# The end of a transformer block's kernel: sums put into PSUM one step sooner, a shorter inverse root, centring read from PSUM

## The chip, the cores and the metric

The kernel runs on one core of one Trainium2 chip. The metric is the device time of one execution in microseconds (us). The kernel before was timed three times: 1820.85 us in the median, 1820.63 us at the lowest and 1821.01 us at the highest. One more execution was taken with the hardware profiler; all rows shown here come from it.

## The reference

256 tokens of width 1024, all in float32, go through two blocks one after the other. The first is a mixer of three attentions and a gated feed-forward layer; the second has two layers: a gated recurrence with a dense feed-forward layer, then differential attention with a mixture of experts. Only the end of the second layer of the second block bears on the change:

```python
y = moe_swiglu(h, w_router, w_gate, w_up, w_down)   # 8 experts, 2 of them for each token
h = layer_norm(DEEPNORM_ALPHA * h + y, ln_g[layer, 1], ln_b[layer, 1])

def layer_norm(x, g, b):
    mu = jnp.mean(x, axis=-1, keepdims=True)
    xc = x - mu
    var = jnp.mean(xc * xc, axis=-1, keepdims=True)
    return xc * lax.rsqrt(var + 1e-5) * g + b
```

An expert computes `(silu(x @ w_gate) * (x @ w_up)) @ w_down` for its tokens, with 3584 hidden features.

## The kernel before, in words

All weights come from HBM as one stream of 1 MB tiles (`wr`, 128 x 2048), in the order in which they are used; SyncE issues the loads (line 266) into slots that the users of earlier tiles set free. The last tile of the stream comes as four loads of 256 KB.

The experts are the last part of the program. Four of them ("heavies", `expert`) have room for 128 tokens, the four others ("lights", `expert_few`, lines 1586 to 1663) for 64. Both kinds run beside each other in a fixed order of turns; what runs last is the last light expert, alone. In the stretch of the experts and the final norm the order of the instructions of TensorE (PE), VectorE (DVE), ScalarE (ACT) and SyncE (SP) is the order in which the code issues them (`manual_schedule(engines=ALL)`), and each engine runs its list in that order.

A light expert goes through seven chunks of 512 hidden features, c = 0 to 6, and one closing round, c = 7:

- gate and up products of chunk c, PSUM bank `gu` (line 1620, 64 matmul records on PE for one chunk), then `hidden` (lines 1414 to 1419): Silu on ACT and a product on DVE, tile `sg`;
- `features` of the chunk before (line 1606): `sg` is turned by PE into PSUM (`uT`), and ACT copies it to `uf` (line 1608). In rounds 1 to 6 this is issued after the first quarter of the gate and up products, in round 7 at the round's start;
- the down product of the chunk before (line 1644, 16 matmul records), added up in bank `dn`.

So round 6 holds the gate and up products of chunk 6 and the down product of chunk 5, and round 7 the down product of chunk 6.

`macc` (128 x 2 x 1024, in SBUF) holds ALPHA times the layer's input plus what all experts gave so far. In the last light expert the sum is closed in PSUM: four matmuls with the identity put the four blocks of 128 x 512 of `macc` into four banks `sum` (lines 1634 to 1639, in round 7 between `features` and the down product). After the down product ACT scales `dn` to `ye` (line 1649), and four matmuls (line 1654, 8 records) add the expert's part into the same banks, each token to its row. DVE takes statistics of each bank (line 1657, `fst`), and ACT copies each bank back to `macc` (line 1658).

`normed` (lines 1710 to 1726) is the final layer norm: `mv` is mean and variance for both token tiles. `inv_sqrt` (lines 440 to 456) computes 1/sqrt(variance + eps) on DVE alone for 128 x 2 values: a first guess by integer operations (lines 446, 447) and three Newton steps of three small instructions each (lines 453 to 455). Between them stand the four centring instructions (line 1717), (macc - mean) * gain, into `done` (a free weight slot, hence `wr` in the trace). Then four instructions multiply by the root and add the bias (line 1724), each followed by a store of 128 x 512 to HBM (line 1726). Gain and bias come by two loads (line 398) into another free weight slot.

If an expert has more tokens than room, a second pass (`again`) runs at the end, and `normed` once more from `macc`. None of its instructions shows in the trace.

Of the kernel before, what the change touches and what calls it, by code (L numbers as in the profile page):

```python
# [10 lines left out]
F32 = mybir.dt.float32  # L11
# [339 lines left out]
def tile_kernel(ctx: ExitStack, tc: tile.TileContext, cst, par, wst, x, mem, g_mix, g_mem, g_ffn, w_forget,  # L351
# [87 lines left out]

    def inv_sqrt(m, eps, between):  # L440


        v, r, w = (mo.tile([128, 2], F32, name=n) for n in ("iv", "ir", "iw"))
        i = mo.tile([128, 2], I32, name="ii")
        V.tensor_scalar(out=v, in0=m, scalar1=eps, scalar2=None, op0=ALU.add)
        V.tensor_scalar(out=i, in0=v.bitcast(I32), scalar1=1, scalar2=None, op0=ALU.logical_shift_right)
        V.tensor_scalar(out=i, in0=i, scalar1=-1.0, scalar2=float(0x5f3759df), op0=ALU.mult, op1=ALU.add)
        r0 = i.bitcast(F32)
        for step in range(4):
            between[step]()  # L450
            if step == 3:
                return r
            V.tensor_tensor(w, r0, r0, op=ALU.mult)
            V.scalar_tensor_tensor(out=w, in0=w, scalar=-0.5, in1=v, op0=ALU.mult, op1=ALU.mult)
            V.scalar_tensor_tensor(out=r, in0=w, scalar=1.5, in1=r0, op0=ALU.add, op1=ALU.mult)
            r0 = r
# [957 lines left out]
    def hidden(pg, pu):  # L1414

        sg = sm.tile([128, 512], F32, name="sg", tag="sq", bufs=2)[:, 0:pg.shape[-1]]
        A.activation(out=sg, in_=pg, func=AF.Silu)
        V.tensor_tensor(sg, sg, pu, op=ALU.mult)
        return sg
# [175 lines left out]
    def expert_few(s, late, last=False):  # L1595
# [15 lines left out]
        for c in range(8):  # L1611
            end = c == 7
            if not end:
# [12 lines left out]
                turn = hidden(ps[:, 0], ps[:, 1])  # L1626
# [6 lines left out]
            if end and last:  # L1633

                for t in range(2):
                    for n in range(2):
                        summed.append(pa("sum"))
                        T.matmul(summed[-1], ident, macc[:, t, n * 512:n * 512 + 512], start=True, stop=False)
# [12 lines left out]
        def scatter(t):  # L1651
            pss = summed[2 * t:2 * t + 2] or [pb("sp") for _ in range(2)]
            for n, h in enumerate(halves):
                T.matmul(pss[n], PT[h, t], y[h], start=not last, stop=True)
            for n in range(2):
                if last:
                    V.bn_stats(out=fst[:, t, n], in_=pss[n])
                    A.activation(out=macc[:, t, n * 512:n * 512 + 512], in_=pss[n], func=AF.Copy)
                else:
                    added(t, n, pss[n], False)  # L1660
# [3 lines left out]
    left = {}  # L1664
# [45 lines left out]
    def normed():  # L1710
# [3 lines left out]

        def centred(t, c):
            cc = slice(c * 512, c * 512 + 512)
            return lambda: V.scalar_tensor_tensor(out=done[:, t, cc], in0=macc[:, t, cc], scalar=mv[:, t, 0:1],
                                                  in1=gbf[:, cc], op0=ALU.subtract, op1=ALU.mult)

        r = inv_sqrt(mv[:, :, 1], 1e-5, [centred(t, c) for t in range(2) for c in range(2)])  # L1720
        for t in range(2):
            for c in range(2):
                cc = slice(c * 512, c * 512 + 512)
                V.scalar_tensor_tensor(out=done[:, t, cc], in0=done[:, t, cc], scalar=r[:, t:t + 1], in1=bbf[:, cc],
                                       op0=ALU.mult, op1=ALU.add)
                nc.sync.dma_start(out=out[t * 128:t * 128 + 128, cc], in_=done[:, t, cc])
# [28 lines left out]
    with tc.manual_schedule(engines=ALL):  # L1755
# [3 lines left out]
        normed()  # L1759

    most = nc.values_load(cint[0:1, 0:1], min_val=0, max_val=S)
    with tc.If(most > 0):
        again()
        with tc.manual_schedule(engines=MS):
            normed()
# [33 lines left out]
```

## Time and profile before

| | |
|---|---|
| median of three runs | 1820.85 us |
| the profiled execution | 1820.72 us |
| its span, first to last instruction or transfer in the trace | 1818.6 us |
| PE busy | 1777.8 us, 98% of the span |
| DVE busy | 1103.4 us, 61% |
| ACT busy | 867.8 us, 48% |
| weights and other data by DMA | 512.70 MB |
| the last instruction on PE ends | about 1803.4 us |
| the last instruction on DVE ends | 1813.05 us |

The profiled execution's own time is 2.12 us more than its span, and 0.13 us under the median of the runs. Engines other than PE are busy for half of the time, so for nearly the whole program they run beside PE. A 128 x 512 product of float32 data shows as two records of PE. "Idle before" in a row is the time in which the engine stood before the instruction, and the name behind the arrow is what ended it.

### The profile page before, as it was taken

The page shows a single profiled execution, that of the slowest core. Times are in us where ns is not written, and L with a number is a line of the kernel's source. Part 1 is how long each engine was busy: PE and PEld are TensorE (multiplying, and loading weights), DVE is VectorE, ACT ScalarE, POOL GpSimd, SP SyncE. Part 2 cuts the span into 40 slices and gives each one's busy share as a digit, 9 for nine tenths or more (in the row PEclk, how much of TensorE's full clock was granted, in tenths as well). Part 3 has the DMA queues.
Part 4 walks back from the last instruction along what each step waited for, and adds up shares of the span by engine and source line. Part 5 has one row for each costly group of instructions (what it writes and reads, how often), then busy time and mean ns, then how long its engine had stood idle before and what let it go on. Part 6 is the DMA issues. An engine that isn't in the chain of part 4 may idle for free.

```text
span 1818.6 us, 27621 instructions
## 1 busy us (share of the span) xinstructions
PE 1777.8 (98%) x11150; PEld 1427.3 (78%) x11150; DVE 1103.4 (61%) x1609; ACT 867.8 (48%) x1222; POOL 0.2 (0%) x4
## 2 busy tenths in 40 slices
PE   8999999999999999999999999999999999999996
PEld 6898998999899899987787767776777677766662
DVE  7856756555676955569789464746464645664622
ACT  6675655444433454436547344545453534553521
POOL 0000000000000000000000000000000000000000
PEclk9999999999999999999999999999999999999998
DMA  7533455555433465534647699999999999999995
GB/s 266 184 140 139 146 193 196 199 206 186 169 137 131 172 235 197 194 140 181 229 173 292 255 420 420 419 420 419 419 419 420 419 419 419 419 419 418 409 419 220
DMA packets 73287, 512.70 MB, mean 282 GB/s; under 512 B 8512, under 2 KB 9152, under 8 KB 12096
## 3 DMA queue, kind: packets, MB, share of 16 engines
q1 hardware_dynamic: 73152, 510.86, 71.2%
q8 instruction: 89, 1.46, 0.3%
q14 instruction: 46, 0.38, 0.1%
HBM read 509.78 MB, written 1.05 MB: 281 GB/s over the span
## 4 chain that ended last, share of the span: by engine, by line
PE 79%; DMA 11%; DVE 7%; ACT 2%; issue 1%; SPq 0%; DVEq 0%; ACTq 0%
DMA wr<-in_wst_dram 10%; PE gu L1620 8%; PE fm L482 7%; PE fm L493 7%; PE fm L486 7%; PE gu L482 5%; PE gu L484 5%; PE gu L491 5%; PE dn L1644 4%; PE acc L484 3%; PE acc L482 3%; PE acc L491 3%; DVE wl L309 3%; PE tk L484 3%; PE tk L482 3%; PE tk L491 3%
## 5 line engine op out<-in xcount | busy, mean ns | idle before, releaser
L309 DVE TENSOR_TENSOR wl<-wr,wh 128x1024 fp32r<-128x1024 f32 x620 | 729.7, 1220 | 366.1 <-ACT wh L307 352.9
L307 ACT ACTIVATE wh<-wr 128x1024 fp32r<-128x1024 f32 x620 | 617.4, 1051 | 315.7 <-PE fm L486 91.3
L482 PE MATMUL fm<-xh,wh 128*128 128x256 f32 x1056 | 251.5, 280 | 0.0
L486 PE MATMUL fm<-xl,wh 128*128 128x256 f32 x1056 | 249.6, 278 | 0.0
L1620 PE MATMUL gu<-wr,xfew 128*64 128x256 f32 x1792 | 208.2, 385 | 0.0
L482 PEld LDWEIGHTS fm<-xh,wh 128*128 128x128 f32 x1056 | 198.8, 188 | 1.1 <-issue 0.2
L486 PEld LDWEIGHTS fm<-xl,wh 128*128 128x128 f32 x1056 | 198.7, 188 | 0.9
L1620 PEld LDWEIGHTS gu<-wr,xfew 128*64 128x64 f32 x1792 | 124.9, 138 | 77.5 <-issue 21.9
L482 PE MATMUL gu<-wh,xe 128*128 128x512 f32 (+1 forms) x448 | 178.3, 399 | 0.0
L484 PE MATMUL gu<-wh,xe 128*128 128x512 f32 (+1 forms) x448 | 173.7, 389 | 0.0
L493 PE MATMUL fm<-xh,wl 128*128 128x256 f32 x1056 | 145.4, 278 | 0.0
L493 PEld LDWEIGHTS fm<-xh,wl 128*128 128x128 f32 x1056 | 131.6, 188 | 0.0
L491 PE MATMUL gu<-wl,xe 128*128 128x512 f32 (+1 forms) x448 | 120.0, 390 | 0.4 <-DVE wl L309 0.4
L482 PE MATMUL tk<-wh,xh 128*128 128x512 f32 x288 | 115.7, 402 | 1.7 <-ACT wh L307 1.5
L484 PE MATMUL tk<-wh,xl 128*128 128x512 f32 x288 | 113.5, 394 | 0.5 <-DVE xl L464 0.5
L482 PEld LDWEIGHTS gu<-wh,xe 128*128 128x128 f32 x448 | 84.5, 189 | 31.7 <-ACT wh L307 11.7
L1608 ACT ACTIVATE uf<-uT 128x256 f32<-128x256 f32 x28 | 10.7, 384 | 203.9 <-PE uT L1606 203.9
L1644 PE MATMUL dn<-wr,uf 128*64 128x512 f32 x448 | 103.0, 594 | 1.9 <-ACT uf L1608 1.4
L491 PEld LDWEIGHTS gu<-wl,xe 128*128 128x128 f32 x448 | 83.6, 189 | 19.2 <-DVE wl L309 1.1
L484 PEld LDWEIGHTS gu<-wh,xe 128*128 128x128 f32 x448 | 84.5, 189 | 16.6 <-DVE xe L464 0.3
L482 PE MATMUL dn<-wh,uh 128*128 128x512 f32 x224 | 89.2, 398 | 0.0
L484 PE MATMUL dn<-wh,ul 128*128 128x512 f32 x224 | 88.0, 393 | 0.0
(347 smaller groups left out, 2214.7 us busy)
## 6 DMA issues: line engine op xcount, KB each, us to landing
wr<-in_wst_dram SPq DMA_DIRECT2D x477, 1024.0 KB, 12.1
gb<-in_ln_g_dram SPq DMA_DIRECT2D x3, 512.0 KB, 5.7
gb<-in_ln_b_dram SPq DMA_DIRECT2D x3, 512.0 KB, 6.5
memt<-in_mem_dram SPq DMA_DIRECT2D x2, 512.0 KB, 7.3
res<-in_x_dram SPq DMA_DIRECT2D x2, 512.0 KB, 12.9
wr<-in_wst_dram SPq DMA_DIRECT2D x4, 256.0 KB, 15.5
out_dram<-wr SPq DMA_DIRECT2D x4, 256.0 KB, 3.0
gb<-in_g_mem_dram SPq DMA_DIRECT2D x1, 512.0 KB, 5.1
```

The lines of the kernel that those rows point to most:

```text
L307: self.nc.scalar.activation(out=h[:, c], in_=t[:, c], func=AF.Copy)
L309: return [lambda c=c: self.nc.vector.tensor_tensor(l[:, c], t[:, c], h[:, c].bitcast(F32), op=ALU.subtract) for c in cols]
L482: T.matmul(ps, ah, bh, start=first and i == 0, stop=False)
L484: T.matmul(ps, al, bh, start=False, stop=False)
L486: T.matmul(ps, ah, bl, start=False, stop=False)
L491: T.matmul(ps, ah, bl, start=False, stop=last and i == n - 1)
L493: T.matmul(ps, al, bh, start=False, stop=last and i == n - 1)
L1608: A.activation(out=U, in_=pT, func=AF.Copy)
L1620: T.matmul(ps[h, g], xfew[:, u + k, i * FEW:i * FEW + FEW], w[:, k, 256 * b:256 * b + 256], start=u + k == 0, stop=u + k == KD - 1)
L1644: T.matmul(acc[h], U[:, j, b * FEW:b * FEW + FEW], wd[n][:, k], start=c == 1 and k == 0, stop=end and k == 3)
```

## The change

Four edits, all at the end of the program.

1. In the last light expert the four identity matmuls that put `macc` into the banks `sum` are issued in round 6, between the gate and up products of chunk 6 and the down product of chunk 5, and no longer in round 7. The first of the four banks comes from the other pool of PSUM (`pb` in place of `pa`), since chunk 6 still holds a bank of `pa`.
2. `hidden` of chunk 6 is followed on ACT by the load of the function table that holds Ln and Exp (`LOGEXP`).
3. The inverse root is exp(-0.5 * ln(v)) by two instructions on ACT, and one Newton step on DVE. The integer guess and two Newton steps go.
4. The four centring instructions read the banks `sum` in place of `macc`, and stand in a row before the Newton step. ACT's four copies of the banks to `macc` come after `normed`.

```diff
--- before.py
+++ after.py
@@ -437,24 +437,6 @@
         V.tensor_tensor(w, w, r, op=ALU.mult)
         return w
 
-    def inv_sqrt(m, eps, between):
-
-
-        v, r, w = (mo.tile([128, 2], F32, name=n) for n in ("iv", "ir", "iw"))
-        i = mo.tile([128, 2], I32, name="ii")
-        V.tensor_scalar(out=v, in0=m, scalar1=eps, scalar2=None, op0=ALU.add)
-        V.tensor_scalar(out=i, in0=v.bitcast(I32), scalar1=1, scalar2=None, op0=ALU.logical_shift_right)
-        V.tensor_scalar(out=i, in0=i, scalar1=-1.0, scalar2=float(0x5f3759df), op0=ALU.mult, op1=ALU.add)
-        r0 = i.bitcast(F32)
-        for step in range(4):
-            between[step]()
-            if step == 3:
-                return r
-            V.tensor_tensor(w, r0, r0, op=ALU.mult)
-            V.scalar_tensor_tensor(out=w, in0=w, scalar=-0.5, in1=v, op0=ALU.mult, op1=ALU.mult)
-            V.scalar_tensor_tensor(out=r, in0=w, scalar=1.5, in1=r0, op0=ALU.add, op1=ALU.mult)
-            r0 = r
-
     def urgent():
 
         return tc.high_priority(offset=PRIO)
@@ -1411,10 +1393,12 @@
         mm3(ps, [((X5[0][:, k, tk], X5[1][:, k, tk]), (w[0][:, k], w[1][:, k])) for k in range(KD)])
         return ps
 
-    def hidden(pg, pu):
+    def hidden(pg, pu, final=False):
 
         sg = sm.tile([128, 512], F32, name="sg", tag="sq", bufs=2)[:, 0:pg.shape[-1]]
         A.activation(out=sg, in_=pg, func=AF.Silu)
+        if final:
+            A.preload_act_table_set(LOGEXP)
         V.tensor_tensor(sg, sg, pu, op=ALU.mult)
         return sg
 
@@ -1623,18 +1607,18 @@
                             U = features(turn)
                         if late and c == 0:
                             late.pop(0)()
-                turn = hidden(ps[:, 0], ps[:, 1])
+                turn = hidden(ps[:, 0], ps[:, 1], last and c == 6)
             else:
                 U = features(turn)
             if c == 0:
                 acc = pb("dn")
             if c == 3:
                 PT, gs = back([[few[:, t, i]] * 2 for t in range(2)], s, F32, "PU")
-            if end and last:
+            if c == 6 and last:
 
                 for t in range(2):
                     for n in range(2):
-                        summed.append(pa("sum"))
+                        summed.append((pb if t + n == 0 else pa)("sum"))
                         T.matmul(summed[-1], ident, macc[:, t, n * 512:n * 512 + 512], start=True, stop=False)
             if c:
                 wd = [W.get_whole(), W.get_whole()]
@@ -1655,13 +1639,13 @@
             for n in range(2):
                 if last:
                     V.bn_stats(out=fst[:, t, n], in_=pss[n])
-                    A.activation(out=macc[:, t, n * 512:n * 512 + 512], in_=pss[n], func=AF.Copy)
+                    sums.append(pss[n])
                 else:
                     added(t, n, pss[n], False)
 
         return [lambda: scatter(0), lambda: scatter(1)]
 
-    left = {}
+    left, sums = {}, []
 
     def heavies(Pm, begun):
         late = []
@@ -1707,23 +1691,25 @@
 
     mv = mo.tile([128, 2, 2], F32, name="mv")
 
-    def normed():
+    def normed(part):
 
         for t in range(2):
             V.bn_aggr(out=mv[:, t], in_=fst[:, t])
-
-        def centred(t, c):
-            cc = slice(c * 512, c * 512 + 512)
-            return lambda: V.scalar_tensor_tensor(out=done[:, t, cc], in0=macc[:, t, cc], scalar=mv[:, t, 0:1],
-                                                  in1=gbf[:, cc], op0=ALU.subtract, op1=ALU.mult)
-
-        r = inv_sqrt(mv[:, :, 1], 1e-5, [centred(t, c) for t in range(2) for c in range(2)])
-        for t in range(2):
-            for c in range(2):
-                cc = slice(c * 512, c * 512 + 512)
-                V.scalar_tensor_tensor(out=done[:, t, cc], in0=done[:, t, cc], scalar=r[:, t:t + 1], in1=bbf[:, cc],
-                                       op0=ALU.mult, op1=ALU.add)
-                nc.sync.dma_start(out=out[t * 128:t * 128 + 128, cc], in_=done[:, t, cc])
+        v, r, w = (mo.tile([128, 2], F32, name=n, tag=n) for n in ("iv", "ir", "iw"))
+        V.tensor_scalar(out=v, in0=mv[:, :, 1], scalar1=1e-5, scalar2=None, op0=ALU.add)
+        A.activation(out=r, in_=v, func=AF.Ln)
+        A.activation(out=r, in_=r, func=AF.Exp, scale=-0.5)
+        cols = [(t, slice(n * 512, n * 512 + 512), part(t, n)) for t in range(2) for n in range(2)]
+        for t, cc, ps in cols:
+            V.scalar_tensor_tensor(out=done[:, t, cc], in0=ps, scalar=mv[:, t, 0:1], in1=gbf[:, cc], op0=ALU.subtract,
+                                   op1=ALU.mult)
+        V.tensor_tensor(w, r, r, op=ALU.mult)
+        V.scalar_tensor_tensor(out=w, in0=w, scalar=-0.5, in1=v, op0=ALU.mult, op1=ALU.mult)
+        V.scalar_tensor_tensor(out=r, in0=w, scalar=1.5, in1=r, op0=ALU.add, op1=ALU.mult)
+        for t, cc, ps in cols:
+            V.scalar_tensor_tensor(out=done[:, t, cc], in0=done[:, t, cc], scalar=r[:, t:t + 1], in1=bbf[:, cc],
+                                   op0=ALU.mult, op1=ALU.add)
+            nc.sync.dma_start(out=out[t * 128:t * 128 + 128, cc], in_=done[:, t, cc])
 
     with tc.manual_schedule(engines=MS):
         tail(0)
@@ -1756,13 +1742,15 @@
         experts(Pm, [s0, s1])
         gbf, bbf = bcast2(W.spare(), 1, 1)
         done = W.spare().rearrange("p (t c) -> p t c", t=2)
-        normed()
+        normed(lambda t, n: sums[2 * t + n])
+        for i, ps in enumerate(sums):
+            A.activation(out=macc[:, i // 2, i % 2 * 512:i % 2 * 512 + 512], in_=ps, func=AF.Copy)
 
     most = nc.values_load(cint[0:1, 0:1], min_val=0, max_val=S)
     with tc.If(most > 0):
         again()
         with tc.manual_schedule(engines=MS):
-            normed()
+            normed(lambda t, n: macc[:, t, n * 512:n * 512 + 512])
 
 
 def arrange(inputs):
```

The list of PE around the end of the last light expert, before (`gu` gate and up products, `uT` the turning of a chunk's features, `dn` the down product, `sum<-macc` the identity matmuls, `sum<-ye` the adding of the expert's part):

```order
L1606 MATMUL uT<-cs,sg 128x128 x2
L1620 MATMUL gu<-wr,xfew 64x256 x24
L1644 MATMUL dn<-wr,uf 64x512 x8
L1606 MATMUL uT<-cs,sg 128x128 x2
L1638 MATMUL sum<-macc,cs 128x512 x4
L1644 MATMUL dn<-wr,uf 64x512 x8
L1654 MATMUL sum<-ye,PU 128x512 x4
```

The same place of PE's list in the changed kernel, where line numbers are 16 lower:

```order
L1590 MATMUL uT<-cs,sg 128x128 x2
L1604 MATMUL gu<-wr,xfew 64x256 x24
L1622 MATMUL sum<-macc,cs 128x512 x4
L1628 MATMUL dn<-wr,uf 64x512 x8
L1590 MATMUL uT<-cs,sg 128x128 x2
L1628 MATMUL dn<-wr,uf 64x512 x8
L1638 MATMUL sum<-ye,PU 128x512 x4
```

The four identity matmuls moved ahead of the first down product shown, past it and past the turning `uT`; nothing else on PE moved, and all that stands earlier in the program is as before.

The end of ACT's list in the changed kernel, from the Silu of chunk 6 on (`ir<-iv` is Ln, `ir<-ir` is Exp):

```order
L1399 ACTIVATE sg<-gu 128x256
L1401 ACT_TABLE_LOAD
L1592 ACTIVATE uf<-uT 128x256
L1633 ACTIVATE ye<-dn,gs 128x512
L1700 ACTIVATE ir<-iv 128x2
L1701 ACTIVATE ir<-ir 128x2
L1747 ACTIVATE macc<-sum 128x512 x4
```

Before, the table load and the two small instructions were not there, and the four copies followed `ye` directly.

## Rows read from the trace of the kernel before

**Rows 1.** The page: span, and busy time of PE with its share and count.

```profile
span 1818.6 us, 27621 instructions
...
PE 1777.8 (98%) x11150; PEld 1427.3 (78%) x11150; DVE 1103.4 (61%) x1609; ACT 867.8 (48%) x1222; POOL 0.2 (0%) x4
```

**Rows 2.** Chain of work that ended last, from 1785 us: start, length, what.

```profile
1772.64 16.88 DMA wr<-in_wst_dram
...
1797.02 3.63 PE dn L1644 x16
```

**Rows 3.** Timeline of the last light expert: start, length, engine, what, count, idle before.

```profile
1775.89 3.60 PE L1644 MATMUL dn<-wr,uf 128*64 128x512 f32 x16
...
1779.42 0.50 PE L1521 MATMUL sp<-yy,PT 128*128 128x512 f32 x1
...
1788.02 1.02 PE L1644 MATMUL dn<-wr,uf 128*64 128x512 f32 x2
1788.65 0.42 DVE L1418 TENSOR_TENSOR sg<-sg,gu 128x256 f32<-128x256 f32 x1 [7.18 <-ACT sg L1417]
1789.56 0.20 PEld L1644 LDWEIGHTS dn<-wr,uf 128*64 128x64 f32 x4 [1.41 <-DMA wr<-in_wst_dram]
...
1793.14 0.44 PE L1606 MATMUL uT<-cs,sg 128*128 128x128 f32 x2
...
1793.42 3.60 PE L1638 MATMUL sum<-macc,cs 128*128 128x512 f32 x8
1793.68 0.38 ACT L1608 ACTIVATE uf<-uT 128x256 f32<-128x256 f32 x1 [5.06 <-PE uT L1606]
...
1796.95 3.65 PE L1644 MATMUL dn<-wr,uf 128*64 128x512 f32 x16
...
1800.68 0.69 ACT L1649 ACTIVATE ye<-dn,gs 128x512 f32<-128x512 f32 x1 [6.61 <-PE dn L1644]
...
1801.41 1.99 PE L1654 MATMUL sum<-ye,PU 64*128 64x512 f32 x8 [0.81 <-ACT ye L1649]
```

**Rows 4.** DMA issue at 1781.96 us: last weights, KB, us to landing.

```profile
wr<-in_wst_dram SPq DMA_DIRECT2D x1, 256.0 KB, 12.7
```

**Rows 5.** Stretches: us, busy time by engine, PE clock granted, DMA share, GB/s.

```profile
1788.00:1793.00 5.00, 4.48 (x18) 1.18 (x15) 0.42 (x1) 0.38 (x1) 0.00 (x0) 1.00 1.02 397
...
1801.00:1804.00 3.00, 1.99 (x8) 0.69 (x8) 1.43 (x3) 1.05 (x3) 0.00 (x0) 1.00 0.02 5
```

**Rows 6.** Timeline of the final norm.

```profile
1802.58 2.49 DVE L1657 BATCH_NORM_STATS2 fst<-sum 128x6 f32<-128x512 f32 x4 [13.50 <-PE sum L1654]
1803.31 2.39 ACT L1658 ACTIVATE macc<-sum 128x512 f32<-128x512 f32 x4 [1.95 <-DVE fst L1657]
...
1805.35 0.17 DVE L445 TENSOR_SCALAR iv<-mv 128x2 f32<-128x2 f32 x1
...
1805.75 0.17 DVE L447 TENSOR_SCALAR ii<-ii 128x2 int32<-128x2 int32 x1
1806.28 0.75 DVE L1717 SCALAR_TENSOR_TENSOR wr<-macc,mv,wr 128x512 f32<-128x512 f32 x1 [0.36 <-issue]
1806.95 0.15 DVE L453 TENSOR_TENSOR iw<-ii 128x2 f32<-128x2 f32 x1
...
1807.33 0.16 DVE L455 SCALAR_TENSOR_TENSOR ir<-iw,ii 128x2 f32<-128x2 f32 x1
1807.41 0.75 DVE L1717 SCALAR_TENSOR_TENSOR wr<-macc,mv,wr 128x512 f32<-128x512 f32 x1
...
1810.32 2.73 DVE L1724 SCALAR_TENSOR_TENSOR wr<-wr,ir 128x512 f32<-128x512 f32 x4
```

**Rows 7.** DVE group by shape: busy us, mean ns, idle before, releaser.

```profile
L1514 DVE SCALAR_TENSOR_TENSOR yy<-dn,gs,yy 128x512 fp32r<-128x512 f32 x8 | 6.0, 751 | 19.0 <-ACT yy L1513 19.0
```

**Rows 8.** Groups of ACT by shape: small functions and table loads.

```profile
L1417 ACT ACT_TABLE_LOAD x2 | 2.6, 1283 | 0.0
...
L428 ACT ACTIVATE nr<-nv 128x1 f32<-128x1 f32 x12 | 2.4, 201 | 26.3 <-DVE nv L427 26.3
```

## The prediction, made before the changed kernel had run

> **What bounds the kernel now.** I read the page first, then the chain of waits at the end, then the timeline of the last 45 us, because the change touches nothing earlier. PE is busy for 98% of the span of 1818.6 us [rows 1]. So the program is bound by PE's list while that list runs, and what comes behind it, on other engines, lies bare on the end. The chain of waits shows both: until 1789.5 us the chain is a weight load, then PE to the end of the last down product (3.63 us from 1797.02 us on) [rows 2], and from there a relay of ACT, PE and DVE with one engine at work at a time. The reader should see in the timeline that the end has three parts: PE's list to about 1800.6 us, the relay over `ye` and the last matmuls to the statistics at 1802.58 us, and DVE alone from there to 1813.05 us [rows 3, 6]. After that come the last store and the closing, 1818.6 - 1813.05 = 5.55 us of the span, which I leave as they are.
>
> **The sums one step sooner (PE).** In round 6 the gate and up products end and the first down matmul starts at 1788.02 us. It stops after one of its eight matmuls, because the second weight tile is not there: PE's weight loading waits for a DMA and goes on at 1789.56 us [rows 3]. The whole down product of round 6 takes 1793.14 - 1788.02 = 5.12 us from its start to the start of what follows, where the same block one round earlier takes 1779.42 - 1775.89 = 3.53 us [rows 3]. So the wait costs 1.59 us. The identity matmuls take 1796.95 - 1793.42 = 3.53 us from start to start [rows 3]. Put at 1788.02 us they run until 1791.55 us, two microseconds beyond the landing of that tile, and the whole wait is covered.
>
> What is lost is the cover that they gave in round 7. There the chunk's turning starts at 1793.14 us, the identity matmuls 0.28 us later, and ACT's copy `uf` (start 0.54 us after the turning's start, 0.38 us long) is done long before the down product needs it at 1796.95 us [rows 3]. In the changed list the down product follows the turning directly and must wait for that copy. The hop from ACT's end to PE's start I take from `ye`: it ends at 1801.37 us and the next matmul starts at 1801.41 us [rows 3], 0.04 us. So turning to down product: 0.54 + 0.38 + 0.04 = 0.96 us, where 0.28 us is all that the turning took before; 0.68 us are added.
>
> New times: sums 1788.02 to 1791.55, down product 1791.55 to 1795.08, turning at 1795.08, last down product at 1796.04 us. Before it started at 1796.95 us, so **0.91 us** are gained (1.59 - 0.68). The last weights are in place: their last load is issued at about 1782 us and lands 12.7 us later, at 1794.7 us [rows 4], 1.3 us ahead of the new start. Bounds of this term: nothing, if the sums cannot start where they now stand (a rival below), and 1.59 us, if the new hop cost nothing.
>
> The table load takes 1.28 us [rows 8]. It stands on ACT between the Silu of chunk 6, whose product DVE starts at 1788.65 us [rows 3], and `uf`, which is not due before 1795.6 us in the new order, so the 7 us of idle ACT hide it. Without that cover it would delay `uf` and so the down product by 1.28 us.
>
> **The root and the centring (DVE).** From `iv` (the variance plus eps) at 1805.35 us to the end of the last instruction at 1810.32 + 2.73 = 1813.05 us DVE needs 7.70 us now [rows 6]. By parts:
> - The two integer instructions: from `iv` to the second of them 1805.75 - 1805.35 = 0.40 us [rows 6]. They go.
> - In front of the first centring DVE stands 0.36 us for nothing that the trace shows [rows 6]. In the list this instruction waits for gain, bias and slot by three DMA signals and for ACT's copy; in the new kernel the three DMA signals remain. I keep the 0.36 us. Bounds: it goes altogether, or stays.
> - Each centring takes 0.67 us until the next instruction starts (1806.28 to 1806.95), each Newton step 0.46 us more (1806.95 to 1807.41) [rows 6]. Four centrings stay. Two Newton steps go, 2 x 0.46 = 0.92 us.
> - The remaining step's third instruction was followed at once by a centring that does not use it, 0.08 us after its start (1807.33 to 1807.41). Now the next instruction uses its result, which costs a whole pitch of small instructions, about 0.19 us (the two between 1806.95 and 1807.33) [rows 6]. Added: 0.11 us.
>
> Sum 0.40 + 0.92 - 0.11 = **1.21 us**.
>
> Ln and Exp lie beside the centrings. `iv` ends at 1805.52 us on the old clock; a small function on ACT takes 0.20 us [rows 8], so with hops of some 0.04 us the root is there about 0.5 us after `iv`. DVE wants it only after four centrings, 0.36 + 4 x 0.67 = 3.0 us after `iv`. There are 2.5 us of slack, more than even a second table load of 1.28 us.
>
> The centrings now read PSUM. The nearest row is the same form of instruction, 128 x 512 with its first input in PSUM: 751 ns [rows 7], against 0.75 us for the centring from SBUF [rows 6]. I take no difference. [...]
>
> ACT's copies to `macc` were waited for by the centrings and now wait for them: that ACT waits for DVE bank by bank shows already before (1.95 us behind the statistics [rows 6]). The last copy starts when the fourth centring ends, some 3.3 us after `iv`, and takes 0.6 us (2.39 us for four [rows 6]); DVE ends 6.5 us after `iv`. So nothing waits for them, unless the output pass became 2.5 us shorter.
>
> **Sum.** 0.91 + 1.21 = 2.12 us less than the profiled execution's 1820.72 us: 1818.6 us. That execution lies 0.13 us under the median of the runs, so I forecast **1818.7 us**, a gain of 0.12%. About 0.2%, 3.6 us, is what a measurement of this kernel can tell from no change, so the forecast lies within it.
>
> **Rivals.**
> - The sums start late. If the first bank `sum` were one that chunk 6 still holds, its first matmul would wait for that chunk's product on DVE, 1788.65 + 0.42 = 1789.07 us [rows 3], that is 1.05 us after its place; the gain of 0.91 us is gone and only the norm gains: 1820.85 - 1.21 + 0.14 = 1819.8 us. Against it: the first bank comes from the other pool, and the other three from banks of earlier chunks. In the same way the gain on PE goes if the last weights land 2 us later than now. Chance 0.08.
> - Only PE gains, the norm does not: if the wait for Ln and Exp outlasted the centrings by 1.2 us, that is, if ACT took 4.2 us for what I put at 0.5. 1820.85 - 0.91 = 1819.9 us. Chance 0.04.
> - More than forecast: the 0.36 us in front of the centring go too, and the hop to the last down product overlaps the turning. 1818.7 - 0.36 - 0.5 = 1817.8 us. To reach 0.2% another 0.6 us would be needed, for which I see no row. Chance 0.12 for clearly more gain, of which a third beyond 0.2%.
> - Slower: PE's clock falls in the new hop. PE now has a gap of some 0.5 us between the turning and the last down product. [...] Against it: through the DMA wait of round 6, which is longer, and through the 0.81 us before the last matmuls the granted clock stays at 1.00 [rows 3, 5]. [...] Chance 0.02.
>
> **How the numbers follow.** The forecast has 0.74: both gains as worked out, within half a microsecond (1818.2 to 1819.3). The range should hold 8 of 10: with the page's price for PSUM, the loss of the DVE gap of 0.36 us, either gain alone (1819.8, 1819.9) and the stronger case (1817.8), it goes from 1817.8 to 1819.9 us. Faster by over 0.2% (below 1817.2 us): 0.05. Slower by over 0.2% (above 1824.5 us) would need the clock rival in full and something besides: 0.01. Within 0.2%: 0.94.
>
> **What would show it.** In the profile after: the DMA wait before the weight loading of round 6 is gone from PE and eight records of identity matmuls stand in its place; the last down product starts about 0.9 us sooner, with a wait for ACT's `uf` of about half a microsecond before it; the table load lies between Silu and `uf`, with ACT idle behind it; Ln and Exp lie under the first centring; DVE goes from `iv` to its end in about 6.5 us with no wait for ACT's root; the four centrings take about 0.75 us each. I am wrong if the sums wait for a bank, if the centrings from PSUM take visibly longer than 0.75 us, or if a wait for ACT appears in front of the Newton step.

## The result: 11 us slower, and none of it where the change is

The changed kernel takes 1832.09 us (median of 5 runs, 1829.50 to 1832.68); the kernel before took 1820.85 us (1820.09 to 1821.08) beside it. The ratio is 1.0059, interval [1.0045, 1.0073]. The forecast was 1818.7 us, so the sign is wrong.

First the page of the kernel after: span, and busy time of PE.

```profile
span 1830.3 us, 27616 instructions
...
PE 1797.8 (98%) x11150; PEld 1438.9 (79%) x11150; DVE 1102.8 (60%) x1601; ACT 866.8 (47%) x1225; POOL 0.2 (0%) x4
```

Beside [rows 1]: PE has the same 11150 matmuls, but they are busy for 1797.8 us instead of 1777.8, 20.0 us more. PE's idle time fell from 1818.6 - 1777.8 = 40.8 us to 1830.3 - 1797.8 = 32.5 us, 8.3 us less. 20.0 - 8.3 = 11.7 us is the whole difference of the spans. The change neither adds nor enlarges a matmul; something made the old ones slower.

**The end, where the change is.** The timeline of the last light expert and of the norm, after (start, length, engine, line, what, count, idle before):

```profile
1802.22 3.70 PE L1622 MATMUL sum<-macc,cs 128*128 128x512 f32 x8
...
1802.74 1.28 ACT L1401 ACT_TABLE_LOAD   x1
...
1805.85 3.65 PE L1628 MATMUL dn<-wr,uf 128*64 128x512 f32 x16
...
1809.44 0.44 PE L1590 MATMUL uT<-cs,sg 128*128 128x128 f32 x2
...
1810.41 3.65 PE L1628 MATMUL dn<-wr,uf 128*64 128x512 f32 x16 [0.53 <-ACT uf L1592]
...
1818.81 0.17 DVE L1699 TENSOR_SCALAR iv<-mv 128x2 f32<-128x2 f32 x1
1818.91 2.73 DVE L1704 SCALAR_TENSOR_TENSOR wr<-sum,mv,wr 128x512 f32<-128x512 f32 x4
1819.01 0.20 ACT L1700 ACTIVATE ir<-iv 128x2 f32<-128x2 f32 x1 [4.18 <-DVE iv L1699]
...
1819.70 2.57 ACT L1747 ACTIVATE macc<-sum 128x512 f32<-128x512 f32 x4 [0.25 <-DVE wr L1704]
...
1821.56 0.15 DVE L1706 TENSOR_TENSOR iw<-ir 128x2 f32<-128x2 f32 x1
...
1822.13 2.74 DVE L1710 SCALAR_TENSOR_TENSOR wr<-wr,ir 128x512 f32<-128x512 f32 x4
```

The reader is to see that the end looks as predicted: the sums run at once, the table load lies under them, Ln stands under the first centring, no wait for ACT stands before the Newton step. From the place where the lists part (down product before, sums after) to DVE's end it was 1813.05 - 1788.02 = 25.03 us [rows 3, 6] and is 1824.87 - 1802.22 = 22.65 us: **2.38 us less**, 2.12 were forecast. But that place is reached 1802.22 - 1788.02 = **14.2 us later**. With 0.1 us less for the closing, 14.2 - 2.4 - 0.1 = 11.7 us.

**Upstream, where it came from.** The loads of ACT's tables mark the same points of the program in both traces. Before, in the timeline of ACT:

```profile
295.43 1.28 ACT L631 ACT_TABLE_LOAD   x1
...
793.94 1.28 ACT L422 ACT_TABLE_LOAD   x1
...
964.56 1.28 ACT L1417 ACT_TABLE_LOAD   x1
```

After:

```profile
298.06 1.28 ACT L613 ACT_TABLE_LOAD   x1
...
807.27 1.28 ACT L422 ACT_TABLE_LOAD   x1
...
978.94 1.28 ACT L1399 ACT_TABLE_LOAD   x1
```

The delay is 2.6 us, then 13.3, then 14.4. It grows with the work of PE, not at one wait. The groups by shape name the work; before (busy us, mean ns of one, idle before):

```profile
L482 PE MATMUL fm<-xh,wh 128*128 128x256 f32 x1056 | 251.5, 280 | 0.0
L486 PE MATMUL fm<-xl,wh 128*128 128x256 f32 x1056 | 249.6, 278 | 0.0
...
L493 PE MATMUL fm<-xh,wl 128*128 128x256 f32 x1056 | 145.4, 278 | 0.0
```

After:

```profile
L464 PE MATMUL fm<-xh,wh 128*128 128x256 f32 x1056 | 257.6, 282 | 0.0
L468 PE MATMUL fm<-xl,wh 128*128 128x256 f32 x1056 | 255.8, 281 | 0.0
...
L475 PE MATMUL fm<-xh,wl 128*128 128x256 f32 x1056 | 149.0, 281 | 0.0
```

These are the gate and up products of the two feed-forward layers, and the same form of product in projections beside them (split inputs `xh`, `xl`, streamed through PE, against weights `wh`, `wl`, loaded into it): 15.9 of the 20.0 us. A block of eight of them in the timeline of PE, before:

```profile
370.99 1.07 PE L493 MATMUL fm<-xh,wl 128*128 128x256 f32 x8
```

and after:

```profile
370.32 1.10 PE L475 MATMUL fm<-xh,wl 128*128 128x256 f32 x8
```

The last record of a block lasts 0.28 us, so seven pitches (a pitch is the time from one product's start to the next) are 0.79 us before (113 ns each) and 0.82 us after (117 ns). From the starts of single records in the feed-forward layers I read 113.3 ns before and 117.3 ns after, in all three groups and with no idle time between. The simplest view of it is how many matmuls fit into a stretch in which PE does the feed-forward's products without a pause. 300 to 460 us, PE's busy time and count in the second and third place, granted clock near the end; before:

```profile
300.00:460.00 160.00, 160.00 (x1175) 150.31 (x1175) 85.17 (x83) 73.81 (x84) 0.00 (x0) 1.00 0.56 202
```

After:

```profile
300.00:460.00 160.00, 160.00 (x1151) 150.19 (x1150) 81.88 (x82) 70.75 (x82) 0.00 (x0) 1.00 0.57 202
```

PE is busy for all 160 us in both, the granted clock is 1.00 in both, DMA moves the same 202 GB/s: 24 matmuls fewer, 2%. This count serves as the mark below.

Of the 8.3 us of PE's idle time that went, 2.4 went ahead of the last of these table loads (13.7 us of idle time before, 11.3 after), 4.2 between it and the place where the lists part (10.6 and 6.4), and 1.8 in the end itself. The largest single piece lies among the experts, between 1640 and 1680 us. That stretch, and PE's timeline at one place in it, before:

```profile
1640.00:1680.00 40.00, 37.38 (x180) 24.18 (x179) 17.99 (x19) 14.34 (x17) 0.00 (x0) 0.91 1.01 419
...
1655.72 2.67 PE L1654 MATMUL sp<-ye,PU 64*128 64x512 f32 x4 [2.15 <-DVE macc L1483]
1658.32 6.05 PE L1620 MATMUL gu<-wr,xfew 128*64 128x256 f32 x32
```

After:

```profile
1640.00:1680.00 40.00, 39.44 (x212) 25.25 (x209) 24.80 (x26) 19.79 (x25) 0.00 (x0) 1.00 1.01 418
...
1673.35 3.67 PE L1604 MATMUL gu<-wr,xfew 128*64 128x256 f32 x32
```

DMA is full at 419 and 418 GB/s (share 1.01 in both); before, PE stood 2.6 us here, after, 0.6. Of the 2.6, 2.15 us are a wait for DVE; before it DVE had stood 13.2 us for ACT, and ACT 1.9 us for a weight load. From 1600 to 1700 us ACT's waits for weight loads add up to 8.7 us before and 2.2 after. So here the later PE waited less for what comes by DMA.

The two stretches differ in one thing more: the mean granted clock is 0.91 before and 1.00 after, and the 32 products behind that wait take 6.05 us before and 3.67 after (granted clock 0.50 from 1658 to 1661 us before, 1.00 from 1673 to 1678 us after). So of the time that the changed kernel makes up here, 2.4 us go with the lower granted clock. The lower clock does not go with the change: the group of these products, `gu<-wr,xfew`, takes 384 or 385 ns a record in the traces of the kernel before and of experiments 5, 8 and 12 below, and 382 ns in those of the changed kernel and of experiments 1, 2, 3, 4, 6, 7 and 10.

**What differs there.** The instructions are the same; their addresses are not. The traces hold no addresses; the compiled programs do. The old root needs an integer tile `ii` (128 x 2, in the pool of the router and the norm, where it takes 32 bytes of each partition). The new root has none, so all that is placed behind this pool lies 32 bytes lower: `xh` at byte 118,464 instead of 118,496, and with it `xl` and what shares their places. The weights `wh`, `wl` stay (`wh` at 43,040). The distance from stationary weights to streamed inputs falls from 75,456 to 75,424 bytes, that is from 192 to 160 modulo 256. The other buffers of `xh`, `xl`, `wh` and `wl` lie multiples of 256 bytes from these.

### The profile page after: what moved, and what is told of

Read it like the earlier page. It is cut to its first block, busy times and chain, and to the rows that moved or that the text cites. A ratio compares the mean times of both kernels' runs of the same rounds, so it can differ in the third digit from the quotient of the medians.

```text
span 1830.3 us, 27616 instructions
## 1 busy us (share of the span) xinstructions
PE 1797.8 (98%) x11150; PEld 1438.9 (79%) x11150; DVE 1102.8 (60%) x1601; ACT 866.8 (47%) x1225; POOL 0.2 (0%) x4
## 4 chain that ended last, share of the span: by engine, by line
PE 92%; DVE 5%; ACT 1%; issue 1%; DMA 0%; SPq 0%; DVEq 0%; ACTq 0%
PE gu L1604 10%; PE fm L464 7%; PE fm L475 7%; PE fm L468 7%; PE gu L464 6%; PE gu L466 6%; PE gu L473 6%; PE dn L1628 5%; PE acc L466 3%; PE acc L464 3%; PE acc L473 3%; PE tk L466 3%; PE tk L473 3%; PE tk L464 3%; PE dn L464 3%; PE dn L473 3%
## 5 line engine op out<-in xcount | busy, mean ns | idle before, releaser
L464 PE MATMUL fm<-xh,wh 128*128 128x256 f32 x1056 | 257.6, 282 | 0.0
L468 PE MATMUL fm<-xl,wh 128*128 128x256 f32 x1056 | 255.8, 281 | 0.0
L473 PEld LDWEIGHTS gu<-wl,xe 128*128 128x128 f32 x448 | 83.6, 189 | 20.8 <-DVE wl L309 0.8
## 6 DMA issues: line engine op xcount, KB each, us to landing
res<-in_x_dram SPq DMA_DIRECT2D x2, 512.0 KB, 12.9
```

What stands on the lines that cost most here:

```text
L464: T.matmul(ps, ah, bh, start=first and i == 0, stop=False)
L468: T.matmul(ps, ah, bl, start=False, stop=False)
L473: T.matmul(ps, ah, bl, start=False, stop=last and i == n - 1)
```

## The experiments

**Theory:** the distance in SBUF between the streamed and the stationary operand sets PE's pitch in these products. **Rivals:** the code itself (other instructions at the end, or where the instructions lie); the absolute address of the inputs; the weights or another tile that moved along. Ratios are against the kernel before, run on the same chip.

**1. The changed kernel with 32 bytes put back.**

```diff
     mv = mo.tile([128, 2, 2], F32, name="mv")
+    mo.tile([128, 8], F32, name="pad")
```

> The changed kernel with 32 unused bytes per partition in the place where the integer tile `ii` of the old root lay, so that every operand of PE lies in SBUF where it lay before; no instruction differs from the changed kernel. Theory A (the loss is a matter of where tiles lie in SBUF: without `ii` all tiles behind it lie 32 bytes lower, and PE's products run slower from there): the slow products are gone, the fm products are back at 113 to 114 ns, and only the gain of the end is left, 25.03 - 22.65 = 2.4 us between the start of the stretch behind the last gate and up products and the end of DVE, so 1820.85 - 2.4 = 1818.4 us (1817.8 to 1819.2). Theory B (the loss comes from the changed instructions or the changed program as such, wherever tiles lie): about 1832 us, as the changed kernel.

Measured: 1818.57 us, ratio 0.9983 [0.9974, 0.9992]; the pitch is 113.3 ns. The stretch of the feed-forward:

```profile
300.00:460.00 160.00, 160.00 (x1183) 150.62 (x1181) 84.35 (x83) 74.31 (x86) 0.00 (x0) 1.00 0.57 206
```

The unused tile takes 13.5 us off the changed kernel, and what is left is the gain at the end. (1183 in place of the 1175 of the kernel before, at the same pitch: the count also goes by which products fall into the stretch.) No instruction differs from the changed kernel's.

**2. The kernel before without its integer tile** (the bits of the root go to an old 8-column tile that is free by then).

```diff
-        i = mo.tile([128, 2], I32, name="ii")
+        i = i8[:, 0, 0:2].bitcast(I32)
```

> The kernel before with nothing changed but that the integer guess of the root is kept in a tile that the routing no longer needs, so that `ii` is not allocated and all tiles behind it lie 32 bytes lower, as in the changed kernel. Theory A (place in SBUF): about 1832.1 + 2.4 = 1834.5 us (1831 to 1836), fm products at 115 to 120 ns. Theory B (the changed instructions): 1820.85 us, within 0.5 us.

Measured: 1834.07 us, ratio 1.0078 [1.0064, 1.0091]; pitch 117.25 ns.

```profile
300.00:460.00 160.00, 160.00 (x1151) 150.19 (x1150) 81.83 (x82) 70.82 (x82) 0.00 (x0) 1.00 0.56 202
```

The same 1151 matmuls as in the changed kernel, with the old end. So no edit at the end is needed for the loss, and the code rival falls.

**3 and 4. Distance or address.** A tile of 32 bytes ahead of all, in the pool of constants, moves weights and inputs alike. In the changed kernel it puts the inputs back to their old addresses and the weights 32 bytes above theirs (the new distance stays); in the kernel before it moves both up (the old distance stays).

```diff
     causb = const.tile([128, 128], BF16, name="causb")
+    const.tile([128, 8], F32, name="pad")
```

Changed kernel:

> The changed kernel with 32 unused bytes per partition ahead of the weight tiles, so that the whole layout behind the constants moves up: the inputs of the products (xh, xl) lie where they lay before, the weight halves (wh, wl) 32 bytes higher than before; the distance between them is that of the changed kernel. Theory A1 (what counts is where the streamed inputs themselves start): 1818.4 us, fm products at 113 to 114 ns. Theory A2 (what counts is the distance between the streamed input and the stationary weights): about 1832 us, fm products at 115 to 120 ns.

Measured: 1831.28 us, ratio 1.0055 [1.0039, 1.0070], 1150 matmuls in the stretch.

Kernel before:

> The kernel before with 32 unused bytes per partition ahead of the weight tiles: inputs and weights of the products all 32 bytes higher, the distance between them as before. Theory A1 (the start of the streamed inputs counts; here it lies 64 bytes above that of the changed kernel): slow, about 1834 us. Theory A2 (the distance counts): 1820.85 us, within 0.7 us. If the step of 32 bytes matters in neither way, also 1820.85 us, and the experiment with the inputs back in place tells the two apart.

Measured: 1820.16 us, ratio 0.9995 [0.9986, 1.0004], 1175 matmuls. Inputs at their old address are slow when the weights have moved, and both moved alike are as fast as ever. The absolute address falls, the distance stands.

**5 and 6. The two halves of the change, each at the old distance.** The sums alone, in the kernel before:

```diff
-            if end and last:
+            if c == 6 and last:
 ...
-                        summed.append(pa("sum"))
+                        summed.append((pb if t + n == 0 else pa)("sum"))
```

> The kernel before with the first edit alone (the identity matmuls in round 6, the first bank from the other pool); the root and the norm as before, and all tiles where they were. By the step of the prediction: the wait of 1.59 us for a weight tile is covered and a hop of 0.68 us is added, so 0.9 us less: 1820.85 - 0.9 = 1820.0 us against 1820.85 us on the same chip, and in the profile the last down product starts 4.6 us after the turning of round 6's end less the sums, that is 8.0 us after the gate and up products end (before: 8.9 us). The rival that the sums start late: no gain, and a gap in front of the first identity matmul.

Measured: 1819.41 us, ratio 0.9987 [0.9978, 0.9997]. The timeline of PE:

```profile
1787.31 3.70 PE L1638 MATMUL sum<-macc,cs 128*128 128x512 f32 x8
...
1795.50 3.65 PE L1644 MATMUL dn<-wr,uf 128*64 128x512 f32 x16 [0.53 <-ACT uf L1608]
```

8.19 us from the sums to the last down product, as in the changed kernel (1802.22 to 1810.41).

The norm alone (the changed kernel with the diff above turned back, and with the 32 bytes of experiment 1):

> The other three edits alone (table load, root by ACT with one Newton step, centring from PSUM), with 32 unused bytes in place of `ii`, so that all tiles lie where they lay before. By the profile of the changed kernel, where DVE needs 24.87 - 18.81 = 6.06 us from `iv` to its end against 7.70 us before: 1.6 us less, 1820.85 - 1.6 = 1819.2 us. The prediction said 1.2 us. If the centring from PSUM or the wait for ACT cost something that the early sums hid, less than 1.2 us.

Measured: 1819.41 us, ratio 0.9991 [0.9979, 1.0002].

```profile
1788.48 3.65 PE L1628 MATMUL dn<-wr,uf 128*64 128x512 f32 x14 [1.35 <-DMA wr<-in_wst_dram]
...
1804.26 0.17 DVE L1700 TENSOR_SCALAR iv<-mv 128x2 f32<-128x2 f32 x1
...
1807.59 2.74 DVE L1711 SCALAR_TENSOR_TENSOR wr<-wr,ir 128x512 f32<-128x512 f32 x4
```

The wait for the second weight tile is back, and from `iv` to the end it is 1807.59 + 2.74 - 1804.26 = 6.07 us, again as in the changed kernel (6.06). The two halves do not touch each other. The intervals, 2 us to either side, are too wide to price them; the sizes come from the traces.

**7 and 8. Is it the alignment to 64 bytes?** The pad of experiment 1 with 64 and 96 bytes (16 and 24 columns; the first is shown): inputs 32 and 64 bytes above their old place.

```diff
-    mo.tile([128, 8], F32, name="pad")
+    mo.tile([128, 16], F32, name="pad")
```

> The changed kernel with 64 unused bytes in the place of `ii`: inputs of the products 32 bytes above where they were before, weights where they were. Theory A2 with a period of 64 bytes (the distance between the two operands has to be a multiple of 64 bytes, as it was before): slow, fm products at 115 to 120 ns, about 1831 us. If only lying lower, or a distance below that of before, were the harm: 1818.5 us, fm products at 113 to 114 ns.

> The changed kernel with 96 unused bytes in the place of `ii`: inputs of the products 64 bytes above where they were before. Theory A2 with a period of 64 bytes: fast, fm products at 113 to 114 ns, 1818.5 us. If only the very distance of before is fast, or the period is longer than 64 bytes: slow, about 1831 us.

Measured: 1832.82 us, ratio 1.0062 [1.0045, 1.0078], 1144 matmuls, pitch 118.3 ns; and 1834.12 us, ratio 1.0065 [1.0048, 1.0083], pitch 120.0 ns. The second one's stretch:

```profile
300.00:460.00 160.00, 160.00 (x1143) 151.33 (x1142) 81.53 (x81) 69.35 (x82) 0.00 (x0) 1.00 0.56 199
```

A period of 64 bytes would have made the last one as fast as the kernel before; it is the slowest of all. That guess falls.

**9. The products alone.** A small kernel whose PE does only such groups (24 products for each half of a bank, split inputs and weights in one buffer), with the inputs moved by 32 bytes from group to group; one execution. Shift 0 is the old distance modulo 256 bytes.

```diff
+SHIFTS = [4096] * 3 + [32 * i for i in range(-8, 25)] + [1024, 2048, 4096, 0]
```

> Not the computation of the reference, but PE's products by themselves: groups of 48 fp32r products of 128 x 256 in the order of the feed-forward layer (streamed xh and xl, stationary wh and wl), read from one tile of SBUF that nothing writes meanwhile; from group to group the streamed inputs start 32 bytes further from the weights, from 256 bytes below to 768 bytes above the distance of the kernel before, then 1024, 2048, 4096 and 0. Theory A3 (PE's own reads of the two operands get in each other's way, by their distance): the groups repeat what the whole kernels showed, 113.3 ns a product at 0, 117.3 at -32, 118.3 at +32, 120.0 at +64 bytes, and the curve shows its period. Theory A4 (the products are held up by what ACT, DVE and the DMAs write into SBUF at the same time): all groups alike, 113.3 ns.

Blocks of eight products in the timeline of PE, where the result's name gives the shift in bytes (m is minus, p plus):

```profile
30.58 1.07 PE L53 MATMUL p4096x<-buf 128*128 128x256 f32 x8
...
32.73 1.07 PE L53 MATMUL m256x<-buf 128*128 128x256 f32 x8
...
43.94 1.12 PE L53 MATMUL m192x<-buf 128*128 128x256 f32 x8
...
78.12 1.10 PE L53 MATMUL p0x<-buf 128*128 128x256 f32 x8
...
89.48 1.12 PE L53 MATMUL p64x<-buf 128*128 128x256 f32 x8
```

PE alone, with no other engine busy and DMA at 1 GB/s (means of 30 to 60 us and of 80 to 120 us), has a pitch that goes by the distance, and from shift -224 on the pattern returns every 256 bytes: -192, 64, 320 and 576 all give 119.8 ns. At 32 and 64 bytes it is near what the whole kernels showed (118.3 and 119.8 ns, there 118.3 and 120.0). What I had not expected: at shift 0 (and 256, 512, 4096 later on) the pitch is 117.8 ns, although the first groups, at 4096 and -256, ran at 113.3 ns; at -32 it is 118.7. So the step of the whole kernels, 113.3 to 117.3 ns, is not repeated here: a good distance alone does not give the short pitch.

**10. A better version: two of the sums in round 6, two in round 7,** with the 32 bytes. Two sums (1.8 us) would cover the wait of 1.59 us, and the other two the copy `uf`.

```diff
-            if c == 6 and last:
+            if c >= 6 and last:
 ...
-                for t in range(2):
-                    for n in range(2):
-                        summed.append((pb if t + n == 0 else pa)("sum"))
 ...
+                t = c - 6
+                for n in range(2):
+                    summed.append(pa("sum"))
 ...
```

> The changed kernel with 32 unused bytes in place of `ii`, and the identity matmuls divided: the two of the first token tile in round 6, the two of the second in round 7 behind the turning, as before the change. Two of them take 1.77 us, so both the wait for the weight tile (1.59 us in the profile of the kernel before) and the hop over ACT (0.68 us) stay covered: 0.7 us less than with all four in round 6, so 1818.57 - 0.7 = 1817.9 us, 3 us (0.16%) under the kernel before. If the weight tile comes late enough to need all four (it did by 1.35 + 0.31 us in one profile), the gain is 0.5 us or less. Either way the last down product starts without a wait for ACT.

Measured: 1817.58 us, ratio 0.9980 [0.9969, 0.9991].

```profile
1787.55 1.98 PE L1622 MATMUL sum<-macc,cs 128*128 128x512 f32 x4
...
1789.46 4.42 PE L1628 MATMUL dn<-wr,uf 128*64 128x512 f32 x16
...
1790.23 0.28 PEld L1628 LDWEIGHTS dn<-wr,uf 128*64 128x64 f32 x4 [0.58 <-DMA wr<-in_wst_dram]
...
1795.90 3.65 PE L1628 MATMUL dn<-wr,uf 128*64 128x512 f32 x16
```

The wait for ACT before the last down product is gone, but the down product of round 6 now starts before its weights are complete (PE's weight loading waits 0.58 us for a DMA) and takes 4.42 us instead of 3.65. It is 8.35 us from the sums to the last down product, against 8.18 in experiment 1 (1787.06 to 1795.24 us): the gain expected over that one is not there.

**11. What selects between 113.3 and 117.8 ns?** The small kernel with a wait of PE for ACT between parts, again one execution (a name's first two letters are part and group): if PE took up a state at each start, a good distance behind a wait would run at 113.3 ns; if the distance of the groups just before decided, only behind a group of another distance would it differ.

```diff
+PARTS = [[0] * 3, [0] * 12, [0, -32, 0, 0, 0], [0, 0], [-64, -64], [-32, -32], [32, 32], [64, 64], ...
```

> Not the computation of the reference, but PE's products by themselves again, in parts with a wait for ACT between them. In the first run of this kind the groups at 4096 and -256 bytes took 113.3 ns a product, those from -224 on 117.7 to 119.9 with a pattern that repeats every 256 bytes, but those at 0, 256, 512, 1024 and 4096 bytes behind them 117.8, though 4096 had been fast at the start. Theory P (the distance decides, with a period of 256 bytes, and once a slow product has shifted the two streams of reads against each other that shift stays until PE stands still): the part of twelve groups at 0 stays at 113.3 ns throughout; 0, -32, 0, 0, 0 goes 113.3, 118, 117.8, 117.8, 117.8; after the next wait 0 is back at 113.3; behind waits of their own -64 to 192 bytes are slow, 256 and 512 bytes are at 113.3. Theory Q (the distance has nothing to do with it here, dense products become slow after some time): within the twelve groups at 0 the products go from 113.3 to 117.8 ns, and 32 bytes make no difference behind a wait.

```profile
34.06 1.10 PE L62 MATMUL ba_p0x<-buf 128*128 128x256 f32 x8
...
164.56 1.10 PE L62 MATMUL fb_m32x<-buf 128*128 128x256 f32 x8
...
180.39 1.12 PE L62 MATMUL ha_p64x<-buf 128*128 128x256 f32 x8
...
201.06 1.09 PE L62 MATMUL ib_p96x<-buf 128*128 128x256 f32 x8
...
228.99 1.10 PE L62 MATMUL la_p256x<-buf 128*128 128x256 f32 x8
```

All groups at 0, 256 and 512 run at 117.8 ns, behind a wait or not, and 113.3 ns does not appear at all. Both guesses fall. Where the good distance runs at its long value it is not even the best: the second group at -32 runs at 117.3 ns and that at 96 at 116.7.

The whole kernels have both values too. In the projections ahead of the first feed-forward layer, blocks of eight products in the timeline of PE, twice the kernel before:

```profile
98.81 1.07 PE L493 MATMUL fm<-xh,wl 128*128 128x256 f32 x8
...
228.77 1.10 PE L493 MATMUL fm<-xh,wl 128*128 128x256 f32 x8
```

and experiment 1 at the place of the first of these:

```profile
100.38 1.10 PE L475 MATMUL fm<-xh,wl 128*128 128x256 f32 x8
```

All three have the good distance, and the first and the third are the same products: 113 ns a product in one execution, 117 in the other. In the kernel before, about half of the projections' groups run at the long value. In the two feed-forward layers every trace with the good distance shows 113.3 ns and never the long value, and at the three other distances tried no trace shows 113.3 ns anywhere. So a good distance allows the short pitch and does not ensure it; what selects it stays open.

**12. The period in the whole kernel.** Experiment 1 with a constant of 256 bytes (`identb`) taken from the pool ahead of the weights to the pool between them and the inputs: the weights lie 256 bytes lower, the distance is 256 larger than the old one.

```diff
-    identb = const.tile([128, 128], BF16, name="identb")
+    identb = mo.tile([128, 128], BF16, name="identb")
```

> The changed kernel with 32 unused bytes in place of `ii` and a tile of 256 bytes moved from ahead of the weight tiles to behind them: the weight halves lie 256 bytes lower than before, the inputs of the products where they lay before, so that the distance is 256 bytes more than before. Theory P, with its period of 256 bytes: fast, fm products at 113.3 ns, 1818.5 us. If only the very distance of the kernel before is fast: slow, 1831 us or more, fm products at 117 to 120 ns.

Measured: 1818.42 us, ratio 0.9980 [0.9966, 0.9995]; pitch 113.3 ns.

```profile
300.00:460.00 160.00, 160.00 (x1175) 150.23 (x1174) 85.46 (x83) 73.48 (x83) 0.00 (x0) 1.00 0.56 201
```

256 bytes more are no loss, 32 more, 64 more or 32 less are. In the feed-forward layers of the whole kernel the pitch goes by the distance modulo 256 bytes: at 192 (kernel before, experiments 1, 4, 5, 6, 10, 12) PE runs at 113.3 ns, at 160 (after, 2, 3) at 117.3, at 224 (7) at 118.3, at 0 (8) at 120.0. The four other multiples of 32 were not tried.

Experiments 1, 10 and 12 lie below both kernels and cannot be told apart from each other.

## Why the prediction was wrong, point by point

- **The step that failed** is the sentence that the timeline of the last 45 us is enough "because the change touches nothing earlier". That holds for the order of the instructions, not for where their operands lie. I counted the two integer instructions that go, 0.40 us, and not the tile they wrote, and so put all that lies ahead of the end at no difference: the tile's 32 bytes shifted the inputs of the products against their weights. That cost 14.2 us of delay at the head of the end (15.2 us against the trace of experiment 1, where the sums start at 1787.06 us), and by the medians 13.5 us (the changed kernel against experiment 1) and 12.9 us (experiment 2 against the kernel before). No rival had it. The one on the slower side (the clock in the new hop) did not come about: the granted clock stays at 1.00 there (1809.5 to 1810.5 us, and from 1810 to 1815 us) and the last down product takes 3.65 us as before. The chance of 0.01 for more than 1824.5 us counts that rival in full: no run shows what a lower clock would cost there, and what the runs showed is a granted clock of 1.00. The old gap that I called the longer one was that of PE's weight loading; PE itself stood 0.52 us there, as long as in the new hop (0.53).
- **The sums, 0.91 forecast, 0.74 measured** (8.93 - 8.19 us). The covered wait, the free bank and the landed weights came as described. The hop over `uf` is 0.97 us (forecast 0.96). What was short is the length of the blocks: the sums take 3.63 us and the down product of round 6 3.59 us, where I had taken 3.53 for both.
- **The root and the centring, 1.21 forecast, 1.64 measured** (7.70 - 6.06 us). From the first centring to the end it went from 6.77 to 5.96 us, 0.81 less: the two Newton steps less the exposed pitch, as worked out. The mis-sized term is the front: the first centring starts 0.10 us after `iv` starts, before it was 0.93 us. With the 0.40 us of the integer instructions went also the 0.36 us that I kept, though the three DMA signals are still there (the last 0.07 us: it now starts before `iv` has ended). So these signals alone were not what held it; which of the old list's waits it was, I did not isolate. That both terms together came to 2.38 us, near the forecast 2.12, is in part luck: the sums gave 0.17 us less than forecast, the norm 0.43 us more.
- **PSUM as the source of the centrings:** four take 2.73 us from PSUM, four instructions of the same form from SBUF 2.74 us. No run shows the price for PSUM that the range of the forecast takes in; what the runs showed in its place is 745 ns for one centring from PSUM (the changed kernel) and 747 ns for one from SBUF (the kernel before).
- **The table load, Ln, Exp and the copies to `macc`** were hidden as forecast; the copies end 1822.27 us, ahead of DVE's end by 2.6 us.

Shown: that 32 bytes of distance make the loss (1 and 2), that it is the distance and not the address (3, 4), that 256 bytes more do no harm (12), and that PE alone has a pitch that goes by the distance with a period of 256 bytes (9). Not shown: the step from 113.3 to 117.3 ns by PE alone. In the whole kernels other tiles moved along with the inputs, by the same bytes; that the streamed inputs count and not one of those rests on 9. Open: why PE should mind, and what, beside the distance, selects the short pitch, in the small kernels and in the projections of the whole ones.

## What to carry to other kernels

A change that adds or drops a tile can move the tiles behind it, as the 32 bytes of `ii` did here; before trusting "nothing earlier is touched", compare the addresses of the matmul operands in both programs. Where a busy PE slows down with the same instructions, the same count and the same clock, count the matmuls in a full stretch of both traces and pad the pool back before blaming the edit. A gain of 2 us at the end of a program is small beside 4 ns (3.5%) on the pitch of its main products.

## What the runs showed of the hardware that was not expected

- In the feed-forward layers of this kernel the pitch of 128 x 256 products in fp32r, streamed from `xh`/`xl` against `wh`/`wl`, depends on the distance of the two operands in SBUF modulo 256 bytes: 113.3 ns at 192, 117.3 at 160, 118.3 at 224, 120.0 at 0, at a granted clock of 1.00 (300 to 460 us).
- The good distance has two values, 113.3 and about 117.7 ns: in the small kernels, and in the projections of the whole ones, where the same products took the one in one execution and the other in another. In the small kernel the whole kernel's worst distance (64 above the good one) is again among the slowest, 119.8 ns.
- The price of the distance was partly given back here: up to the head of the end PE was busy for 20.8 us more and stood 6.6 us less, so that 14.2 us arrived there. In the stretch of the experts shown above, where DMA is full (418 and 419 GB/s, share 1.01), a wait of 2.15 us was gone.
